# RMSNorm scale applied after the first products of a three-term float32 matmul kernel, and a wider transpose of its gated output

## The chip, the cores and the metric

The kernel runs on one core of one Trainium2 chip. The metric is the device time of one execution in microseconds (us). TensorE (PE) multiplies, VectorE (DVE) and ScalarE (ACT) work on tiles, GpSimd (POOL) and SyncE (SP) mostly issue DMAs here.

## The reference

One gMLP layer and a final RMSNorm on x of 1024 tokens x 2048 channels, all float32 (E = 4096):

```
h = rmsnorm(x, a_norm)
z = h @ w_in                       # 2048 x 12288 -> u | v | gate
u = gelu(u);  v = rmsnorm(gelu(v), v_gain)
sv = w_s mixes the 128 tokens of each chunk, 8 channel groups of 512, + b_s
x = x + (u * sv * silu(gate)) @ w_out      # 4096 x 2048
out = rmsnorm(x, final_norm)
```

## The kernel before

Both big products are Strassen products of 2x2 blocks: seven products p, each with a left factor from `A_OF` and a right one from `B_OF` (a block, or a sum or difference of two). Block 21 is half 1 of the tokens, column half 1, and so on. A float32 factor is split (L85) into hi (ACT rounds it to fp32r) and lo (DVE, the rest), and a product is three matmuls (L91: hi*hi, hi*lo, lo*hi).

The output columns of w_in come in 12 strips of two 512-column blocks: four for v, then eight with u and gate of one group. A strip has seven chains (one per p) of four steps; a step is 24 matmuls of 128x512 (two 128-rows of the inner dimension, four 128-token tiles, three terms), so a strip has 672. Then w_out: seven chains for each of two column pairs, eight steps each. The list `steps` sets this order on PE. At step i the program issues the loads of step i+3 and the sums and splits of step i+2 (`advance`, L367), so DVE and ACT run up to two steps ahead. Whatever a finished chain still needs goes into the lists `soon` and `later` and is popped a few at each step (`work`, L219). A scheduler then settles each engine's order; engines run their queues in order. Tiles come from pools of fixed size (`SLOTS`): a DMA or an instruction that writes a slot waits until its last reader is done.

The first strip makes the left factors for all strips from x and stores hi and lo to DRAM (`a_dram`); later strips load them. Before its first product, `load_x(0)` loads half of x (eight tiles of 512 KB), ACT squares it, DVE adds, a matmul with ones sums over channels, and `scale_x` makes 1/rms, a diagonal matrix of it, and by one more matmul the row `r_b`, by which (and by `g_in`) DVE multiplies each x tile in `h_block` (L171). The same for the other half follows after the first steps. Two chains accumulate into one set of PSUM banks (2 and then 4 and 7; 5 and then 3 and 6), of two sets; `end_of` (L414) takes a chain's banks over.

In a u-and-gate strip `apply_spatial` (L318) mixes the tokens, and `finish_y` (L346) transposes the gated result in 32x32 blocks, four 32-partition transposes for each 32 tokens of a chunk (L354), and stores y as [128, 4, tokens] per group and half. w_out's first column pair loads y, sums and splits it.

Of the kernel before, what the change touches and what calls it, by code (L numbers as in the profile page):

```python
# [10 lines left out]
ALU = mybir.AluOpType  # L11
# [12 lines left out]
FIRST_ORDER = (5, 3, 1, 2, 4, 6, 7)  # L24
# [8 lines left out]
def gmlp_kernel(ctx, tc, x, xT, g_in, w_in, gain, wsT, bsT, w_out, fnorm, out):  # L33
# [11 lines left out]
    NV = G // 2  # L45
    AHEAD, LOADS = 2, 3
# [30 lines left out]
    rx = const([P, NCH], "rx")  # L77
# [37 lines left out]
    y_dram = [[dram.tile([P, CB, HT], F32, tag=f"y{g}_{h}", name=f"y{g}_{h}") for h in range(2)] for g in range(G)]  # L115
# [45 lines left out]
    normal = set()  # L161

    def h_block(step, block, us=(0, 1)):

        key = ((block % 10 - 1) * JI + step[3], block // 10 - 1)
        t = hx[key]
        for u in us:
            if key + (u,) not in normal:
                normal.add(key + (u,))
                k = key[0] * 2 + u  # L170
                nc.vector.scalar_tensor_tensor(  # L171
                    out=t[:, u], in0=t[:, u], scalar=g_sb[:, k:k + 1], in1=r_b[:, key[1]],
                    op0=ALU.mult, op1=ALU.mult)
        return t

    def feed_first():

        step = steps[0]
        (a1, _, a2), (b1,) = A_OF[step[2]], B_OF[step[2]]
        aparts[0] = [slot("ax", f"a_{l}", F32R) for l in ("hi", "lo")]  # L180
        wparts[0] = [slot("hl", f"w_{l}", F32R) for l in ("hi", "lo")]
        split(load_w(step, b1), *wparts[0])
        hs = slot("sum", "a_sum")
        for u in range(2):
            t1, t2 = h_block(step, a1, (u,)), h_block(step, a2, (u,))
            nc.vector.tensor_tensor(out=hs[:, u], in0=t1[:, u], in1=t2[:, u], op=ALU.add)
            split(hs[:, u], *[t[:, u] for t in aparts[0]])
        for t, d in zip(aparts[0], a_dram[step[2], 0]):
            nc.gpsimd.dma_start(out=d, in_=t.bitcast(F32))

    def feed(i):
# [4 lines left out]
        first = kind == "in" and s == 0  # L196
        if first or (kind == "out" and s == 0):
            load = h_block if first else load_y
            raw = combine(A_OF[p], lambda b: load(step, b), "sum", "a_sum")


            out_j = j if kind == "out" else -1
            tag = "big" if (p == OUT_ORDER[0] and out_j >= JO - 4) or (p == OUT_ORDER[-1] and out_j == JO - 1) else "ax"
# [11 lines left out]

# [12 lines left out]

    ones = slot("ax", "ones")
# [4 lines left out]
    ss_x, r_ps = bank_set(1, "ss_x")  # L234
    r_b = slot("sum", "r_b")
    d_x = slot("ax", "d_x")
    dv = d_x.rearrange("p a (b c) -> p a b c", c=P)
    eyes = eye.rearrange("p (a c) -> p a c", a=1).broadcast_to([P, HCH, P])
    order_x = [jj for j in range(JI) for jj in (j, JI + j)]

    def load_x(h):

        for n, jj in enumerate(order_x):
            t = hx[jj, h] = slot("big", "x_t")
            nc.sync.dma_start(
                out=t, in_=xT[jj * 2 * P:(jj + 1) * 2 * P, h * HT:(h + 1) * HT].rearrange("(u p) c -> p u c", p=P))
            sq = slot("ax", "sq_x")
            nc.scalar.activation(out=sq, in_=t, func=AF.Square)
            nc.vector.tensor_tensor(out=sq[:, 0], in0=sq[:, 0], in1=sq[:, 1], op=ALU.add)
            nc.tensor.matmul(out=ss_x[:, h], lhsT=ones[:, 0, :P], rhs=sq[:, 0], start=n == 0, stop=n == len(order_x) - 1)  # L250

    def scale_x(h):

        cs = slice(h * HCH, (h + 1) * HCH)

        nc.vector.tensor_tensor(
            out=dv[:, h], in0=ss_x[:, h].rearrange("p (b c) -> p b c", c=P), in1=eyes, op=ALU.mult)
        nc.vector.tensor_reduce(out=ss_t[:, cs], in_=dv[:, h], axis=mybir.AxisListType.X, op=ALU.add)
# [3 lines left out]
        for n in range(HCH):
            nc.vector.tensor_scalar(
                out=dv[:, h, n], in0=eye, scalar1=rx[:, h * HCH + n:h * HCH + n + 1], scalar2=None, op0=ALU.mult)
        nc.tensor.matmul(out=r_ps[:, h], lhsT=ones[:, 0, :P], rhs=d_x[:, h], start=True, stop=True)
        nc.scalar.activation(out=r_b[:, h], in_=r_ps[:, h], func=AF.Copy)

    load_x(0)
    for i in range(LOADS):
        prefetch(i)  # L270
    scale_x(0)
# [18 lines left out]
    Q = 32  # L290
# [25 lines left out]
    def apply_spatial(g, half, n_set, prod):  # L316
# [29 lines left out]
    def finish_y(g, half, m, i, y):  # L346

        t, c = divmod(m, 2)
        if c == 0 and i == 0:
            yts[0] = slot("ax", "y_t").rearrange("p a (b c) -> p (a b) c", c=2 * P)  # L350
        yt = yts[0]
        yv = y[:, c].rearrange("t (b q c) -> t b q c", b=CB, q=P // Q)
# [4 lines left out]
        if c == 1 and i == P // Q - 1:  # L357
            nc.gpsimd.dma_start(out=y_dram[g][half][:, :, 2 * t * P:2 * (t + 1) * P], in_=yt)  # L358
            pairs_of_y[0] += 1

    pairs_of_y = [0]


    def products(i, banks, fresh, ms=range(4)):
# [263 lines left out]
```

## Time and profile before

| | us |
|---|---|
| median of 3 runs (2563.18 to 2563.37) | 2563.28 |
| profiled execution | 2561.8 |
| its span, first to last instruction | 2560.0 |
| PE busy / DVE / ACT / POOL in the span | 2514.0 / 1797.8 / 856.3 / 167.3 |

The profile counts an overlapping, pipelined PE as busy from the first matmul to the last of a run, so 98% hides slow stretches; the distance between the starts of matmuls shows those. The mean granted clock of TensorE was 0.995.

### The profile page before, as it was taken

The page shows a single profiled execution, that of the slowest core. Times are in us where ns is not written, and L with a number is a line of the kernel's source. Part 1 is how long each engine was busy: PE and PEld are TensorE (multiplying, and loading weights), DVE is VectorE, ACT ScalarE, POOL GpSimd, SP SyncE. Part 2 cuts the span into 40 slices and gives each one's busy share as a digit, 9 for nine tenths or more (in the row PEclk, how much of TensorE's full clock was granted, in tenths as well). Part 3 has the DMA queues.
Part 4 walks back from the last instruction along what each step waited for, and adds up shares of the span by engine and source line. Part 5 has one row for each costly group of instructions (what it writes and reads, how often), then busy time and mean ns, then how long its engine had stood idle before and what let it go on. Part 6 is the DMA issues. An engine that isn't in the chain of part 4 may idle for free.

```text
span 2560.0 us, 29690 instructions
## 1 busy us (share of the span) xinstructions
PE 2514.0 (98%) x10980; PEld 2062.0 (81%) x10980; DVE 1797.8 (70%) x2469; ACT 856.3 (33%) x1008; POOL 167.3 (7%) x290
## 2 busy tenths in 40 slices
PE   7999999999999999999999999999999999999998
PEld 4878888888888888888888888888888788888886
DVE  7974544545448869588595886958769855576795
ACT  4542332323324242232423324233243232232342
POOL 1210000000000000000000000000010110010010
PEclk8999999999999999999999999999999999999999
DMA  8897785958767685766858668586696875678885
GB/s 316 315 411 286 274 313 201 381 204 329 281 254 272 230 336 200 288 260 241 328 203 294 253 242 336 194 307 248 223 362 209 298 257 173 223 263 284 298 294 189
DMA packets 246784, 695.62 MB, mean 272 GB/s; under 512 B 21472, under 2 KB 21488, under 8 KB 246640
## 3 DMA queue, kind: packets, MB, share of 16 engines
q1 hardware_dynamic: 207552, 551.62, 59.7%
q0 software_dynamic: 39088, 142.11, 15.0%
q8 instruction: 87, 1.43, 0.2%
q14 instruction: 57, 0.47, 0.1%
HBM read 622.34 MB, written 71.30 MB: 271 GB/s over the span
## 4 chain that ended last, share of the span: by engine, by line
PE 76%; DVE 16%; issue 5%; DMA 2%; ACT 1%; POOL 0%; SPq 0%; POOLq 0%; ACTq 0%; DVEq 0%
PE m L94 19%; PE m L93 18%; PE m L95 18%; DVE y_t L354 8%; PE o L94 7%; PE o L93 7%; PE o L95 7%; DVE w_lo L89 3%; DVE w_sum L103 1%; DMA w_raw<-in_w_in 1%; DVE c L325 1%; DMA y_raw<-y 1%; DVE u L431 0%; DVE c L411 0%; ACT w_hi L88 0%
## 5 line engine op out<-in xcount | busy, mean ns | idle before, releaser
L93 PE MATMUL m<-w_hi,a_hi 128*128 128x512 f32 x2688 | 1048.5, 390 | 9.4 <-DVE u L431 4.8
L94 PE MATMUL m<-w_lo,a_hi 128*128 128x512 f32 x2688 | 1049.4, 390 | 4.5 <-DVE w_lo L89 4.5
L95 PE MATMUL m<-w_hi,a_lo 128*128 128x512 f32 x2688 | 1047.9, 390 | 0.2 <-DVE a_lo L89 0.2
L89 DVE TENSOR_TENSOR w_lo<-w_sum,w_hi 128x1024 fp32r<-128x1024 f32 x320 | 391.1, 1222 | 402.9 <-ACT w_hi L88 402.0
L88 ACT ACTIVATE w_hi<-w_sum 128x1024 fp32r<-128x1024 f32 x320 | 339.0, 1060 | 954.2 <-PE m L94 668.9
L93 PEld LDWEIGHTS m<-w_hi,a_hi 128*128 128x128 f32 x2688 | 505.8, 188 | 117.8 <-issue 6.6
L94 PEld LDWEIGHTS m<-w_lo,a_hi 128*128 128x128 f32 x2688 | 505.8, 188 | 114.8 <-DVE w_lo L89 9.8
L95 PEld LDWEIGHTS m<-w_hi,a_lo 128*128 128x128 f32 x2688 | 505.6, 188 | 105.8 <-DVE a_lo L89 0.9
L103 DVE TENSOR_TENSOR w_sum<-w_raw 128x1024 f32<-128x1024 f32 x320 | 389.7, 1222 | 100.5 <-DMA w_raw<-in_w_in 88.3
L94 PE MATMUL o<-w_lo,a_hi 128*128 128x512 f32 x896 | 349.6, 390 | 6.0 <-DVE w_lo L89 6.0
L93 PE MATMUL o<-w_hi,a_hi 128*128 128x512 f32 x896 | 348.7, 389 | 0.8 <-DVE o L575 0.8
L95 PE MATMUL o<-w_hi,a_lo 128*128 128x512 f32 x896 | 348.7, 389 | 0.0
L354 DVE STREAM_TRANSPOSE y_t<-c 32x128 f32<-32x128 f32 x1024 | 309.9, 303 | 15.1
L88 ACT ACTIVATE w_hi<-w_raw 128x1024 fp32r<-128x1024 f32 x128 | 135.9, 1061 | 451.2 <-PE m L94 348.7
L89 DVE TENSOR_TENSOR w_lo<-w_raw,w_hi 128x1024 fp32r<-128x1024 f32 x128 | 155.6, 1216 | 132.8 <-ACT w_hi L88 131.9
L94 PEld LDWEIGHTS o<-w_lo,a_hi 128*128 128x128 f32 x896 | 168.2, 188 | 44.0 <-DVE w_lo L89 9.3
L93 PEld LDWEIGHTS o<-w_hi,a_hi 128*128 128x128 f32 x896 | 168.2, 188 | 36.4 <-DVE o L575 1.5
L95 PEld LDWEIGHTS o<-w_hi,a_lo 128*128 128x128 f32 x896 | 168.2, 188 | 34.7
L88 ACT ACTIVATE a_hi<-a_sum 128x1024 fp32r<-128x1024 f32 (+1 forms) x61 | 63.7, 1044 | 146.4 <-DVE a_sum L103 137.0
L143 POOL DMA_DIRECT2D y_raw<-y x96 | 50.9, 531 | 467.0 <-DVE w_sum L103 245.6
L89 DVE TENSOR_TENSOR a_lo<-a_sum,a_hi 128x1024 fp32r<-128x1024 f32 (+1 forms) x61 | 73.3, 1202 | 10.1 <-ACT a_hi L88 10.1
L358 POOL DMA_DIRECT2D y<-y_t x32 | 23.1, 721 | 727.5 <-DVE y_t L354 727.5
(91 smaller groups left out, 1108.2 us busy)
## 6 DMA issues: line engine op xcount, KB each, us to landing
w_raw<-in_w_in SPq DMA_DIRECT2D x212, 512.0 KB, 6.7
w_raw<-in_w_out SPq DMA_DIRECT2D x192, 512.0 KB, 6.4
y_raw<-y POOLq DMA_DIRECT2D x96, 512.0 KB, 6.3
a_hi<-a_0h SPq DMA_DIRECT2D x77, 512.0 KB, 4.9
a_lo<-a_0l SPq DMA_DIRECT2D x77, 512.0 KB, 5.5
a_hi<-a_1h SPq DMA_DIRECT2D x77, 512.0 KB, 6.4
a_lo<-a_1l SPq DMA_DIRECT2D x77, 512.0 KB, 5.1
a_hi<-a_2h SPq DMA_DIRECT2D x77, 512.0 KB, 6.0
```

The source lines that it names most:

```text
L88: nc.scalar.activation(out=hi, in_=raw, func=AF.Copy)
L89: nc.vector.tensor_tensor(out=lo, in0=raw, in1=hi.bitcast(F32), op=ALU.subtract)
L93: nc.tensor.matmul(out=acc, lhsT=ah, rhs=bh, start=start, stop=False, skip_group_check=on)
L94: nc.tensor.matmul(out=acc, lhsT=ah, rhs=bl, start=False, stop=False, skip_group_check=on)
L95: nc.tensor.matmul(out=acc, lhsT=al, rhs=bh, start=False, stop=stop, skip_group_check=on)
L103: nc.vector.tensor_tensor(out=s, in0=a, in1=b, op=ALU.add if of[1] > 0 else ALU.subtract)
L143: nc.gpsimd.dma_start(out=yraw[key], in_=y_dram[g][block // 10 - 1][:, b:b + 2, :])
L325: nc.vector.scalar_tensor_tensor(out=y, in0=sv, scalar=bs_sb[:, g:g + 1], in1=y, op0=ALU.add, op1=ALU.mult)
L354: nc.vector.transpose(out=yt[q * Q:(q + 1) * Q, :, c * P + i * Q:c * P + (i + 1) * Q], in_=yv[i * Q:(i + 1) * Q, :, q, :])
L358: nc.gpsimd.dma_start(out=y_dram[g][half][:, :, 2 * t * P:2 * (t + 1) * P], in_=yt)
```

## The change

1. First strip: x is no longer multiplied by 1/rms. The left factors carry only `g_in` (ACT with a scale per partition, DVE scalar_tensor_tensor). 1/rms of a token (`rx`, one value per partition of a finished block) is the scale of the activation in `act`, which becomes two calls of 128x512 instead of one of 128x1024, in every strip. The squares are summed on DVE over 128x1024 and one matmul per half sums over partitions; the second half of x is loaded and squared during steps 2 to 13 (`first_step`).
2. The first strip runs the chains of one PSUM set in a row (5, 3, 6, then 1, 2, 4, 7), and blocks 11 and 21 of w are kept for several chains: 24 loads instead of 36.
3. `finish_y` transposes 128 partitions x 256 columns at once, two for each chunk; y lands in DRAM by channel, in eight DMAs of 128 KB per group and half (512-byte runs) instead of two of 512 KB. Tokens come out in another order; `split_y` puts them right while splitting, in runs of 32.

```diff
-FIRST_ORDER = (5, 3, 1, 2, 4, 6, 7)
+FIRST_ORDER = (5, 3, 6, 1, 2, 4, 7)
...
+    def split_y(raw, hi, lo):
+        rv_, hv = [t.rearrange("p u (q m t) -> p (u q) m t", m=HCH, t=Q) if t is raw else
+                   t.rearrange("p a b -> p (a b)").rearrange("p (m n t) -> p n m t", m=HCH, t=Q) for t in (raw, hi)]
+        nc.scalar.activation(out=hv, in_=rv_, func=AF.Copy)
...
+        nc.vector.tensor_tensor(out=lm, in0=rm, in1=hm.bitcast(F32), op=ALU.subtract)
...
-        cached = kind == "in" and (s > 0 or block == 22)
+        cached = kind == "in" and (s > 0 or block in (21, 22) or (block == 11 and p in (1, 2, 4)))
...
+    def feed_x(i):
+        step = steps[i]
...
+        if len(of) > 1 and of[0] % 10 != of[2] % 10:
+            raw2, hs = hx[key(of[2])], slot("sum", "a_sum")
+            for u in range(2):
+                nc.scalar.activation(out=hs[:, u], in_=raw2[:, u], func=AF.Copy, scale=g_of(of[2], u))
                 nc.vector.scalar_tensor_tensor(
+                    out=hs[:, u], in0=raw[:, u], scalar=g_of(of[0], u), in1=hs[:, u], op0=ALU.mult, op1=ALU.add)
...
+            for u in range(2):
+                nc.scalar.activation(out=hi[:, u], in_=raw[:, u], func=AF.Copy, scale=g_of(of[0], u))
+                nc.vector.scalar_tensor_tensor(
+                    out=lo[:, u], in0=raw[:, u], scalar=g_of(of[0], u), in1=hi[:, u].bitcast(F32),
+                    op0=ALU.mult, op1=ALU.subtract)
...
+    def square_x(jj, h):
+        sq = slot("ax", "sq_x")
+        nc.scalar.activation(out=sq, in_=hx[jj, h], func=AF.Square)
+        if h in sums:
+            nc.vector.tensor_tensor(out=sums[h], in0=sums[h], in1=sq, op=ALU.add)
...
+    def first_step(i):
+        if 2 <= i < 10:
+            load_x((i - 2), 1)
+        for h, at in enumerate((0, 8)):
+            n = i - at
+            for k in ((n,) if 0 <= n < 4 else (2 * n - 4, 2 * n - 3) if 4 <= n < 6 else ()):
+                square_x(order_x[k] if h == 0 else k, h)
+            if n == 6:
+                scale_x(h, h)
+    for j in range(JI):
+        load_x(j, 0)
+        load_x(JI + j, 0)
+        if j < LOADS:
+            prefetch(j)
...
-    def finish_y(g, half, m, i, y):
...
-        for q in range(P // Q):
-            nc.vector.transpose(
-                out=yt[q * Q:(q + 1) * Q, :, c * P + i * Q:c * P + (i + 1) * Q],
-                in_=yv[i * Q:(i + 1) * Q, :, q, :])
+    def finish_y(g, half, m, y):
...
+        for n in range(2):
+            nc.vector.transpose(out=yts[0][n][:, :, m * Q:(m + 1) * Q], in_=yv[:, n])
+        if m == HCH - 1:
+            yd = y_dram[g][half].rearrange("(n b c) t -> n c b t", n=2, c=Q)
+            for n in range(2):
+                for q in range(P // Q):
+                    nc.gpsimd.dma_start(out=yd[n, :, :, q * P:(q + 1) * P], in_=yts[0][n][q * Q:(q + 1) * Q])
...
-            nc.scalar.activation(out=d, in_=src, func=AF.Gelu_apprx_tanh if is_v or n == 0 else AF.Silu)
+            for c in range(2):
+                at = 2 * t + c
+                nc.scalar.activation(
+                    out=d[:, c], in_=src[:, c], func=AF.Gelu_apprx_tanh if is_v or n == 0 else AF.Silu,
+                    scale=rx[half][:, at:at + 1])
...
-                work()
+                if s == 0:
+                    first_step(i)
+                work(2.3 if s else 1.4)
```

The order on SP's DMA queue at the program's start, before (x_t are tiles of x, w_raw blocks of w_in, a_hi and a_lo the stored left factors; xN is N in a row):

```order
1 L245 DMA x_t<-in_xT 128x2x512 x8
2 L131 DMA w_raw<-in_w_in 128x2x512 x3
3 L245 DMA x_t<-in_xT 128x2x512 x8
4 L131 DMA w_raw<-in_w_in 128x2x512 x35
5 L155 DMA a_hi<-a_0h 128x1024
```

and now:

```order
1 L251 DMA x_t<-in_xT 128x2x512 x2
2 L144 DMA w_raw<-in_w_in 128x2x512
3 L251 DMA x_t<-in_xT 128x2x512 x2
4 L144 DMA w_raw<-in_w_in 128x2x512
5 L251 DMA x_t<-in_xT 128x2x512 x2
6 L144 DMA w_raw<-in_w_in 128x2x512
7 L251 DMA x_t<-in_xT 128x2x512 x2
8 L144 DMA w_raw<-in_w_in 128x2x512 x3
9 L251 DMA x_t<-in_xT 128x2x512
10 L144 DMA w_raw<-in_w_in 128x2x512
```

The loads of the first product's factors are now the first three, and half 1 of x comes between the loads of later steps.

DVE in the middle of the first strip, where it adds the squares of half 1 (sq_x, L259), folds the sum's halves (L266) for the one matmul that sums over channels, and prepares steps 15 to 17 (w_lo, a_lo; u is the take-over of chain 1), now:

```order
83 L259 TENSOR_TENSOR sq_x<-sq_x 128x1024
84 L186 SCALAR_TENSOR_TENSOR a_sum<-x_t,g_sb,a_sum 128x512
85 L259 TENSOR_TENSOR sq_x<-sq_x 128x1024
86 L90 TENSOR_TENSOR w_lo<-w_raw,w_hi 128x1024
87 L90 TENSOR_TENSOR a_lo<-a_sum,a_hi 128x1024
88 L266 TENSOR_TENSOR sq_x<-sq_x 128x512
89 L186 SCALAR_TENSOR_TENSOR a_sum<-x_t,g_sb,a_sum 128x512 x2
90 L271 TENSOR_TENSOR sq_x<-ss_x_0_953,ones 128x512
```

and PE at the matmul that waits for row 88 (ss_x), now:

```order
367 L105 MATMUL m_0_815<-w_hi,a_lo 128x512
368 L103 MATMUL m_1_816<-w_hi,a_hi 128x512
369 L104 MATMUL m_1_816<-w_lo,a_hi 128x512
370 L105 MATMUL m_1_816<-w_hi,a_lo 128x512
371 L268 MATMUL ss_x_0_953<-sq_x,ones 128x512
372 L103 MATMUL m_1_816<-w_hi,a_hi 128x512
```

Before, the sums of squares of half 1 stood much earlier on PE, within the first steps (step 1 of 28):

```order
36 L95 MATMUL m_1_332<-w_hi,a_lo 128x512
37 L250 MATMUL ss_x_168<-sq_x,ones 128x512
38 L94 MATMUL m_1_332<-w_lo,a_hi 128x512
39 L95 MATMUL m_1_332<-w_hi,a_lo 128x512
40 L93 MATMUL m_1_332<-w_hi,a_hi 128x512
41 L94 MATMUL m_1_332<-w_lo,a_hi 128x512
42 L250 MATMUL ss_x_168<-sq_x,ones 128x512 x7
```

So 369 of the first strip's 672 products now stand ahead of the second sum, and one matmul makes it.

DVE in the first u-and-gate strip, where the transposes begin (c is the gated product, sv the mixed tokens), before:

```order
387 L89 TENSOR_TENSOR w_lo<-w_sum,w_hi 128x1024
388 L325 SCALAR_TENSOR_TENSOR c_0_5561<-sv_0_0_5668,bs_sb,c_0_5561 128x512 x2
389 L325 SCALAR_TENSOR_TENSOR c_1_5562<-sv_0_1_5669,bs_sb,c_1_5562 128x512 x2
390 L354 STREAM_TRANSPOSE y_t<-c_0_5561 32x4x32 x16
391 L89 TENSOR_TENSOR v_lo<-v_raw,v_hi 128x1024
392 L89 TENSOR_TENSOR w_lo<-w_sum,w_hi 128x1024
393 L103 TENSOR_TENSOR w_sum<-w_raw 128x1024
394 L354 STREAM_TRANSPOSE y_t<-c_0_5561 32x4x32 x5
```

and now (the last rows of eight transposes in a row, 383 to 390):

```order
389 L376 STREAM_TRANSPOSE y_t_5736<-c_1_5586 128x8x32
390 L376 STREAM_TRANSPOSE y_t_5737<-c_1_5586 128x8x32
391 L90 TENSOR_TENSOR v_lo<-v_raw,v_hi 128x1024
392 L113 TENSOR_TENSOR w_sum<-w_raw 128x1024
393 L90 TENSOR_TENSOR w_lo<-w_sum,w_hi 128x1024
394 L483 TENSOR_TENSOR u_4853<-u_4853,m_0_4992 128x1024
```

The 64 transposes of half a group, which stood in runs between the other work, are eight in one run.

## Rows read from the trace of the kernel before

**Rows 1.** Stretches: us; busy PE, PEld, DVE, ACT, POOL; granted clock; DMA share; GB/s.
```profile
0.00:31.00 31.00, 12.92 (x18) 3.67 (x18) 15.38 (x25) 14.09 (x14) 3.73 (x10) 0.84 0.97 355
31.00:203.30 172.30, 166.01 (x690) 132.08 (x691) 154.00 (x163) 80.75 (x99) 36.05 (x65) 0.97 0.93 350
...
800.00:1900.00 1100.00, 1095.54 (x4819) 903.10 (x4818) 842.10 (x1445) 349.83 (x368) 37.32 (x60) 1.00 0.72 263
1900.00:2060.00 160.00, 153.95 (x671) 124.85 (x670) 143.55 (x226) 54.04 (x55) 23.71 (x39) 1.00 0.78 273
```
**Rows 2.** PE in order of time: start, us, line, tiles, [idle before <- what ended it].
```profile
31.10 0.79 PE L93 MATMUL m<-w_hi,a_hi 128*128 128x512 f32 x1 [4.06 <-ACT a_hi L88]
32.12 0.63 PE L93 MATMUL m<-w_hi,a_hi 128*128 128x512 f32 x1
32.54 0.63 PE L95 MATMUL m<-w_hi,a_lo 128*128 128x512 f32 x1
...
203.31 0.39 PE L93 MATMUL m<-w_hi,a_hi 128*128 128x512 f32 x1
...
355.63 0.39 PE L93 MATMUL m<-w_hi,a_hi 128*128 128x512 f32 x1
...
872.70 0.39 PE L93 MATMUL m<-w_hi,a_hi 128*128 128x512 f32 x1
873.70 0.50 PE L94 MATMUL m<-w_lo,a_hi 128*128 128x512 f32 x1 [0.62 <-DVE w_lo L89]
```
**Rows 3.** What PE waited for: us in total, times, longest us.
```profile
PE ss_x L250 <- DVE sq_x L249: 7.7, 6, 6.3
PE ss_x L265 <- DVE d_x L263: 7.1, 2, 6.4
PE o L94 <- DVE w_lo L89: 6.0, 6, 2.0
PE m L94 <- DVE w_lo L89: 4.5, 7, 0.7
```
**Rows 4.** ACT at the start, each waiting for the next 512 KB tile to land.
```profile
6.09 1.06 ACT L248 ACTIVATE sq_x<-x_t 128x1024 f32<-128x1024 f32 x1 [0.59 <-DMA x_t<-in_xT]
7.58 1.06 ACT L248 ACTIVATE sq_x<-x_t 128x1024 f32<-128x1024 f32 x1 [0.44 <-DMA x_t<-in_xT]
...
18.30 1.06 ACT L88 ACTIVATE w_hi<-w_raw 128x1024 fp32r<-128x1024 f32 x1 [0.30 <-DMA w_raw<-in_w_in]
19.65 1.06 ACT L88 ACTIVATE w_hi<-w_raw 128x1024 fp32r<-128x1024 f32 x1 [0.30 <-DMA w_raw<-in_w_in]
```
**Rows 5.** Granted clock (the number after POOL) around a stall, by stretch.
```profile
31.00:34.60 3.60, 3.50 (x8) 2.66 (x9) 3.60 (x7) 0.67 (x2) 0.64 (x1) 0.50 1.05 386
35.00:38.00 3.00, 3.00 (x14) 2.43 (x14) 3.00 (x5) 0.67 (x1) 0.54 (x1) 1.00 1.06 392
```
**Rows 6.** DVE in order of time: back-to-back instructions in the first strip.
```profile
69.92 1.41 DVE L171 SCALAR_TENSOR_TENSOR x_t<-x_t,g_sb,r_b 128x512 f32<-128x512 f32 x2
...
90.75 2.49 DVE L279 TENSOR_TENSOR c<-c,gain_b 128x512 f32<-128x512 f32 x4
...
118.83 2.35 DVE L89 TENSOR_TENSOR a_lo<-x_t,a_hi 128x1024 fp32r<-128x1024 f32 x2
```
**Rows 7.** Groups of instructions: tiles, count | busy us, mean ns of one | idle before.
```profile
L354 DVE STREAM_TRANSPOSE y_t<-c 32x128 f32<-32x128 f32 x1024 | 309.9, 303 | 15.1
L404 ACT ACTIVATE c<-m 128x1024 f32<-128x1024 f32 x48 | 48.9, 1019 | 56.2 <-PE m L95 56.2
L250 PE MATMUL ss_x<-sq_x,ones 128*128 128x512 f32 x32 | 18.1, 695 | 7.7 <-DVE sq_x L249 7.7
L358 POOL DMA_DIRECT2D y<-y_t x32 | 23.1, 721 | 727.5 <-DVE y_t L354 727.5
L531 ACT ACTIVATE o<-o,ro 128x512 f32<-128x512 f32 x16 | 10.7, 715 | 7.5 <-POOL ro L84 7.5
```
**Rows 8.** DVE at the start of w_out, waiting for y.
```profile
2014.69 1.23 DVE L103 TENSOR_TENSOR a_sum<-y_raw 128x1024 f32<-128x1024 f32 x1 [4.40 <-DMA y_raw<-y]
```

More of the change, by code (lines that the diff above doesn't have):

```diff
@@ L76, in gmlp_kernel @@
     ss_t = const([P, NCH], "ss_t")
-    rx = const([P, NCH], "rx")
+    rx = [const([P, HCH], f"rx{h}") for h in range(2)]
     m_all = const([P, NCH], "m_all")
@@ L114, in gmlp_kernel @@
     v_dram = [[dram.tile([P, HCH, C], F32, tag=f"v{g}_{h}", name=f"v{g}_{h}") for h in range(2)] for g in range(G)]
[L115 removed]
+    y_dram = [[dram.tile([C, HT], F32, tag=f"y{g}_{h}", name=f"y{g}_{h}") for h in range(2)] for g in range(G)]
     a_dram = {(p, j): [dram.tile([P, 2, HT], F32, tag=f"a{p}_{j}{l}", name=f"a{p}_{j}{l}") for l in "hl"]
@@ L195, in feed @@
         kind, s, p, j = step = steps[i]
[L196 to L203, printed above, removed]
+        if kind == "in" and s == 0:
+            feed_x(i)
+        elif kind == "out" and s == 0:
+            raw = combine(A_OF[p], lambda b: load_y(step, b), "sum", "a_sum")
+            tag = "big" if (p == OUT_ORDER[0] and j >= JO - 4) or (p == OUT_ORDER[-1] and j == JO - 1) else "ax"
             parts = [slot(tag, f"a_{l}", F32R) for l in ("hi", "lo")]
-            split(raw, *parts)
+            split_y(raw, *parts)
             aparts[i] = parts
-            if first:
-                for t, d in zip(parts, a_dram[p, j]):
-                    nc.gpsimd.dma_start(out=d, in_=t.bitcast(F32))
         elif kind == "out":
@@ L252, in scale_x, with load_x @@
-    def scale_x(h):
+    order_x = [jj for j in range(JI) for jj in (j, JI + j)]
+    sums = {}
+    def load_x(jj, h):
+        t = hx[jj, h] = slot("big", "x_t")
+        nc.sync.dma_start(
+            out=t, in_=xT[jj * 2 * P:(jj + 1) * 2 * P, h * HT:(h + 1) * HT].rearrange("(u p) c -> p u c", p=P))
+    def square_x(jj, h):
[3 more added lines that the diff above has]
+            nc.vector.tensor_tensor(out=sums[h], in0=sums[h], in1=sq, op=ALU.add)
+        else:
+            sums[h] = sq
@@ new lines, in scale_x @@
+    def scale_x(h, n_set):
+        sq = sums[h]
+        nc.vector.tensor_tensor(out=sq[:, 0], in0=sq[:, 0], in1=sq[:, 1], op=ALU.add)
+        ss_x = bank_set(n_set, f"ss_x{h}")[0]
+        nc.tensor.matmul(out=ss_x[:, 0], lhsT=ones[:, 0, :P], rhs=sq[:, 0], start=True, stop=True)
+        dv = sq[:, 1].rearrange("p (b c) -> p b c", c=P)
+        nc.vector.tensor_tensor(
+            out=dv, in0=ss_x[:, 0].rearrange("p (b c) -> p b c", c=P),
+            in1=eye.rearrange("p (a c) -> p a c", a=1).broadcast_to([P, HCH, P]), op=ALU.mult)
@@ L262, in scale_x @@
[L262 to L271, printed above, removed]
+        nc.gpsimd.tensor_tensor(out=rx[h], in0=m_all[:, cs], in1=mhalf[:, cs], op=ALU.pow)
@@ L327, in apply_spatial @@
         for m in range(HCH):
-            for part in range(P // Q):
-                later.append((1.2, lambda m=m, part=part: finish_y(g, half, m, part, prod[m // 2])))
+            later.append((0.8, lambda m=m: finish_y(g, half, m, prod[m // 2][:, m % 2])))
     def spatial_step(k, g, cs, n_set):
@@ L376, in advance @@
         feed(i + AHEAD)
-    feed_first()
-    for i in range(1, AHEAD):
+    for i in range(AHEAD):
         feed(i)
-    load_x(1)
-    scale_x(1)
     i = 0
@@ L432, in end_of, with last @@
                         out=cs["u"][t], in0=cs["u"][t], in1=banks[t], op=ALU.subtract)))
+                    if s == 0:
+                        def last(t=t):
+                            nc.vector.tensor_tensor(out=cs[22][t], in0=cs[22][t], in1=cs["u"][t], op=ALU.add)
+                            act(22, t, cs[22][t])
+                        soon.append((1.2, last))
+                elif s == 0 and p == 6:
+                    if t == 0:
+                        cs[22] = [slot("ax", f"c22_{t}") for t in range(2)]
+                    soon.append((0, lambda t=t: nc.scalar.activation(out=cs[22][t], in_=banks[t], func=AF.Copy)))
                 elif p in (4, 3):
```

105 lines of the change are left out of this document (40 added, 65 removed).

## The prediction

> **What bounds the kernel now.** I read the busy table by stretch first, then PE in order of time, then PE's waits, then ACT and DVE at the start.
>
> The busy table [rows 1] shows PE nearly full after 203.3 us: idle 1100.00 - 1095.54 = 4.5 us over most of the u-and-gate strips and 160.00 - 153.95 = 6.1 where w_out begins. DVE and ACT are far from full, so on PE nothing but the start and a few late tiles is to be had. PE in order of time [rows 2] gives the scale: strip 1 runs from 203.31 to 355.63, 152.3 us for 672 products, 0.2267 each, 5.44 a step. The first product starts at 31.10 and strip 1 only at 203.31, so the first strip takes 172.2 instead of 152.3. Up to there 203.3 - 152.3 = 51.0 us are lost; that is the big store. PE's waits [rows 3] name the small one: 4.5 us in 7 waits in the strips and 6.0 in 6 waits at w_out, all for a w_lo that DVE made late.
>
> **The start.** The factors of the first product are now the first three loads; three tiles of 512 KB have landed at 7.58, and from there they come 1.35 apart (18.30 to 19.65 [rows 4]). ACT then makes w_hi (1.06, as in rows 4) and half of a_hi (about 0.6, half of it and a little more): first product at about 9.5. The wait for sums, scale and row falls away. [...]
>
> **The first strip, by three sums.**
> PE alone: 9.5 + 1.9 + 152.3, and two sums of squares at 18.1 / 16 = 1.1 each [rows 7] (sixteen now): 165.9.
>
> DVE: PE can't pass the second sum of squares before DVE's row 88 in the order, the last of 55 operations of 128x1024, 34 of scalar_tensor_tensor, nine of 128x512 and two small ones. Back to back they come 1.13, 0.67 and 0.62 apart (from runs of two, two and four [rows 6]); the two small ones I put at 0.7 together: 62.2 + 22.8 + 5.6 + 0.7 = 91.3. DVE can begin when x's second tile is there (6.09 [rows 4]) and ACT has scaled half of it (0.715 [rows 7]), at 6.8, and reaches row 88 at 98.1 plus whatever it idles, I. Behind that matmul stand 303 of 672 products, 68.7 us, and its own 1.1: the strip ends at 167.9 + I. PE would be there at 9.5 + 1.9 + 369 x 0.2267 + 1.1 = 96.1, so it waits there for 2 + I, with everything after it queued behind.
>
> DMA gives I. By the order the loads up to step 11's pair are 30 tiles, and by then about 20 tiles of left factors are stored: 50 tiles, of which 11 have landed at 19.65; 39 x 1.35 = 52.7, so the pair lands at 72.3. Sum, hi and lo (1.13 + 1.06 + 1.13) make its w_lo 75.6. Without idling DVE would have been through that row at 6.8 + 59.1 = 65.9. So I is up to 9.7 if all these stores go first, and 0 if they lag behind the loads. ACT's extra work (two scaled copies of at most 0.715 a step) may add some, since it hands tiles back and forth with DVE; I allow 13. I take 8, nearer to the DMA sum, because the DMA share was already 0.97 in both early stretches [rows 1]. The strip ends at 175.9 instead of 203.3: 27.4 us less. After step 12 loads fall to one or none a step (the kept blocks), so the DMA can't hold the rest.
>
> The chains now follow each other on one bank set at 5-3, 3-6, 2-4 and 4-7. ACT or DVE reads the first banks while PE still writes the last ones, so I count nothing; at most the reading of one bank pair, 1.0 each [rows 7], if ACT is late. That belongs to I.
>
> **The activations in halves.** 96 calls of 1.02 (48 stand in rows 7) become 192 of at most 0.715, the price of half a tile with a scale per partition [rows 7]: up to 96 x 0.41 = 39 us on ACT, busy a third of the span. A chain's banks are needed again only a chain later (four steps, 21.8 us) outside the first strip, so it costs nothing there; with that cover gone it would be 0.4 us a call.
>
> **The transposes.** 1024 of 0.303 us [rows 7], 310 us, become 128. The trace has none of 128 x 256. From below it can't cost less than 0.30, the same instruction with half the columns; from above, eight times as many 32x32 blocks at the same price each make 2.42. I take twice 0.303, since each partition has twice the columns: 0.61, 78 us in all, 232 off DVE. Only the late w_lo tiles turn that into time. Each such wait costs a little more than it shows: 872.70 to 873.70 is 1.00, 0.77 over the pace, for a wait of 0.62 [rows 2]. So 4.5 + 6.0 + 13 x 0.15 = 12.5 us are at stake. The longest (2.0) comes after DVE waited 4.40 for y from DRAM [rows 8], and may stay: 10.5. The eight transposes in one run take 4.9 us before the next w_lo; with two steps of lead, 10.9, PE doesn't see them.
>
> **Stores and splits of y.** POOL issues 128 DMAs instead of 32, at most 0.72 each [rows 7]: 69 us more, on an engine busy 61 us in these stretches [rows 1]. If the 512-byte runs take the DMA twice as long, 16.8 MB at 263 GB/s [rows 1] become 64 us more over 1250, on a share of 0.72. No PE work waits for either, since y is read strips later, except at the end of the last group; I count 0, and 3 us there at worst. The 56 splits that reorder tokens cost 1.13 each if runs of 32 are as good as one run; a bound above is 2.37 ns per column, the transposes' price, 2.42. Then DVE would need 1.3 more in each of 56 steps, which are 5.44 long and hold five operations; some 10 us would come out at PE. I take 0, as all of DVE's rows on plain elementwise work lie at one price per column. [...]
>
> **The sum.** 2560.0 - 27.4 - 10.5 = 2522.1 for the span; the execution lies 1.8 above its span, and the median of the runs 1.5 above the profiled one: about 2525.
>
> **Rivals.**
> *The first strip stays short of tiles.* For it: DMA share 0.97 there, and five tiles a step in steps 8 to 11. With I = 25 it ends at 193, 10 us earlier; with 10.5 from the transposes, 2543. Against it: 12 loads fewer in the strip, and after step 12 one a step or none.
> *The w_lo waits stay or come back elsewhere.* Runs of eight could be late where sixteen short ones were not: only the start's 27.4 remains, 2536. Against it: at w_out, where the longer waits are, DVE is busy 143.6 of 160 us [rows 1], and the transposes are what goes from it.
> *The transposes cost by the block.* At 2.42 the DVE total stays 310 us, but in runs of eight: 19.4, with the four gating operations ahead and the next sum and split behind some 25.5 us without a w_lo, where PE has the step it is in and two more, 16.3. It would stall about 9 us for each of sixteen halves, 147, and end near 2563 - 27 + 147 = 2683: slower. It decides from 8t + 6.1 > 16.3, t = 1.3 us. All transposes in the trace have 32 partitions, so no row excludes it; but DVE's other operations take 128 partitions at 1.1 to 1.2 ns a column [rows 6], under the 2.4 of a transpose of 32, so partitions cost it nothing elsewhere: 0.04. [...]
>
> **How the numbers follow.** Forecast 0.71, with its own range 2515 (I = 0 and all 12.5 back) to 2534 (I = 13, 7 back); strip short of tiles 0.13; waits stay 0.12; by the block 0.04. The range goes down to 2512 (PE's own sum, 165.9, with all 12.5 back and part of the 1.9 for the clock) and up to 2543, the first rival's time, half of which lies beyond; it leaves out about 0.15. A median within 0.2% (5 us) of 2563 counts as no change: only a strip that gains nothing and waits that stay would give that, 0.01. Faster 0.95, slower 0.04.
>
> **What would show it.** First product at 9 to 11 us; strip 1's first product at 168 to 181; a PE wait for the sum of squares (L266) near 96 to 106 us; DVE idle before w tiles between 20 and 75; transposes at about 0.6; no PE wait for w_lo after 800 us but one at w_out. I am wrong if strip 1 starts after 190, if a transpose takes over 1.3 us, or if PE waits anew in the u-and-gate strips.

## The result, and the profile after

| | before | after |
|---|---|---|
| median, us | 2563.32 (2563.18 to 2564.04) | 2527.68 (2527.18 to 2528.85) |
| span of the profiled execution, us | 2560.0 | 2525.5 |
| first product of the program, us | 31.10 | 10.49 |
| first product of strip 1, us | 203.31 | 184.25 |
| from there to the last product, us | 2345.9 | 2329.3 |
| from the last product to the end, us | 10.7 | 11.9 |

The ratio is 0.9861, 95% interval 0.9844 to 0.9878: faster by 35.6 us, where 2525 was forecast and 2527.7 lies within the range. The two terms behind it did not come out as written. The first strip gave 19.1 us and not 27.4, the later strips and w_out 16.6 and not 10.5; the tail took 1.2 back. 19.1 + 16.6 - 1.2 = 34.5 is the difference of the spans. The 19.1 is all start: the first product comes 20.6 us earlier, and from it to strip 1 it takes 173.8 us where it took 172.2. The forecast had the strip itself at 166.4.

The busy table of the kernel after answers [rows 1]; its columns are the same, the granted clock stands behind POOL.

```profile
10.50:16.90 6.40, 6.40 (x14) 4.75 (x15) 5.66 (x7) 4.19 (x6) 1.67 (x3) 1.00 1.04 383
...
34.00:37.30 3.30, 3.30 (x9) 2.55 (x8) 3.30 (x5) 2.51 (x5) 1.90 (x4) 0.50 1.05 395
65.00:71.70 6.70, 0.08 (x1) 0.00 (x0) 5.71 (x5) 3.62 (x5) 5.21 (x2) 0.73 1.04 408
71.70:74.90 3.20, 3.16 (x8) 2.48 (x9) 1.42 (x2) 3.20 (x6) 0.54 (x1) 0.50 1.05 390
...
800.00:1900.00 1100.00, 1100.00 (x4855) 911.14 (x4854) 624.63 (x671) 370.38 (x435) 80.48 (x142) 1.00 0.74 266
1900.00:2060.00 160.00, 160.00 (x708) 132.53 (x707) 108.02 (x101) 52.80 (x58) 33.29 (x58) 1.00 0.81 279
```

Below, PE is full: 1100.00 of 1100 and 160.00 of 160, where it lacked 4.5 and 6.1. DVE fell from 842 to 625 us in the long stretch. Above, PE stands still from 65.0 to 71.7, and the granted clock is 0.50 (half clock below), as in [rows 5], from 34.0 to 37.3 and behind the standstill. In the first row products start 0.43 us apart, as they do from 34.3 to 36.9 at 0.50, though the granted clock of the first row is 1.00.

PE in order of time, and then what it waited for, answer [rows 2, 3].

```profile
10.49 0.80 PE L103 MATMUL m<-w_hi,a_hi 128*128 128x512 f32 x1 [10.49 <-ACT a_hi L89]
...
32.15 0.49 PE L103 MATMUL m<-w_hi,a_hi 128*128 128x512 f32 x1 [1.88 <-ACT a_hi L89]
...
40.33 0.46 PE L103 MATMUL m<-w_hi,a_hi 128*128 128x512 f32 x1
...
43.93 0.50 PE L103 MATMUL m<-w_hi,a_hi 128*128 128x512 f32 x1 [1.52 <-ACT u L447]
...
71.74 0.79 PE L103 MATMUL m<-w_hi,a_hi 128*128 128x512 f32 x1 [6.66 <-ACT c L428]
...
184.25 0.39 PE L103 MATMUL m<-w_hi,a_hi 128*128 128x512 f32 x1
```
```profile
PE m L103 <- ACT a_hi L89: 12.4, 2, 10.5
PE m L103 <- ACT c L428: 6.7, 1, 6.7
PE m L103 <- ACT u L447: 1.5, 1, 1.5
PE o L103 <- DVE o L611: 0.8, 1, 0.8
PE m L105 <- DVE a_lo L90: 0.6, 1, 0.6
PE m L103 <- DVE u L457: 0.2, 1, 0.2
```

Both lines on w_lo are gone, and both on the sums of squares. Chain 3 takes over chain 5's first banks at 40.33 and the others at 43.93. The largest wait behind the start is new: at 71.74 chain 6 wants the bank set of chain 3, which ACT still reads. The next rows are of three engines around that wait, POOL, then DVE, then ACT.

```profile
65.71 4.68 POOL L278 TENSOR_TENSOR rx<-m_all,mhalf 128x4 f32<-128x4 f32 x1
...
119.21 1.05 POOL L278 TENSOR_TENSOR rx<-m_all,mhalf 128x4 f32<-128x4 f32 x1
```
```profile
64.78 0.16 DVE L276 TENSOR_SCALAR m_all<-ss_t 128x4 f32<-128x4 f32 x1
64.86 1.22 DVE L113 TENSOR_TENSOR w_sum<-w_raw 128x1024 f32<-128x1024 f32 x1
65.99 1.22 DVE L195 TENSOR_TENSOR a_sum<-x_t 128x1024 f32<-128x1024 f32 x1
67.13 1.22 DVE L113 TENSOR_TENSOR w_sum<-w_raw 128x1024 f32<-128x1024 f32 x1
68.26 1.22 DVE L90 TENSOR_TENSOR w_lo<-w_sum,w_hi 128x1024 fp32r<-128x1024 f32 x1
69.51 1.23 DVE L195 TENSOR_TENSOR a_sum<-x_t 128x1024 f32<-128x1024 f32 x1
```
```profile
67.24 1.28 ACT L428 ACT_TABLE_LOAD   x1
70.42 2.42 ACT L428 ACTIVATE c<-m,rx 128x512 f32<-128x512 f32 x4 [1.90 <-POOL rx L278]
```

Read them upwards: PE waits for the activation of block 12, that for 1/rms of half 0, and that is POOL's power of 4 numbers a partition. The same instruction took 1.05 us for half 1, beside an operation of DVE that reads one operand from PSUM (u, from 118.36). Here DVE ran operations with two operands from SBUF, back to back, beside it.

Of the groups in [rows 7], the transposes and their stores now read:

```profile
L376 DVE STREAM_TRANSPOSE y_t<-c 128x256 f32<-128x256 f32 x128 | 43.6, 406 | 0.0
L381 POOL DMA_DIRECT2D y<-y_t x128 | 74.0, 586 | 409.1 <-DVE y_t L376 405.4 <-issue 1.9 <-DVE w_lo L90 1.8
```

310 us of transposes became 44.

### The profile page after: what moved, and what is told of

It reads as the page before. It is cut to its first block, busy times and chain, and to the rows that moved or that the text cites. A ratio compares the mean times of both kernels' runs of the same rounds, so it can differ in the third digit from the quotient of the medians.

```text
span 2525.5 us, 28995 instructions
## 1 busy us (share of the span) xinstructions
PE 2491.7 (99%) x10948; PEld 2058.9 (82%) x10948; DVE 1526.9 (60%) x1560; ACT 896.0 (35%) x1144; POOL 221.1 (9%) x386
## 3 DMA queue, kind: packets, MB, share of 16 engines
q0 software_dynamic: 40624, 142.12, 15.2%
## 4 chain that ended last, share of the span: by engine, by line
PE 96%; issue 2%; POOL 1%; DVE 0%; DMA 0%; ACT 0%; SPq 0%; POOLq 0%; ACTq 0%
PE m L103 24%; PE m L104 23%; PE m L105 23%; PE o L103 8%; PE o L105 8%; PE o L104 8%; PE sv L104 1%; PE sv L105 1%; PE sv L103 1%; DMA x_t<-in_xT 0%; POOL rx L278 0%; DVE w_sum L113 0%; DVE w_lo L90 0%; ACT w_hi L89 0%; ACT sq_o L536 0%
## 5 line engine op out<-in xcount | busy, mean ns | idle before, releaser
L381 POOL DMA_DIRECT2D y<-y_t x128 | 74.0, 586 | 409.1 <-DVE y_t L376 405.4
L428 ACT ACTIVATE c<-m,rx 128x512 f32<-128x512 f32 x96 | 60.4, 683 | 55.9 <-PE m L105 54.0
L96 ACT ACTIVATE a_hi<-a_sum 128x1024 fp32r<-128x1024 f32 x40 | 42.3, 1058 | 100.0 <-DVE a_sum L113 100.0
L319 POOL DMA_DIRECT2D v_raw<-v x32 | 17.4, 544 | 661.3 <-DVE ws_hl L334 646.0
```

The source lines that it names most:

```text
L96: nc.scalar.activation(out=hv, in_=rv_, func=AF.Copy)
L319: nc.gpsimd.dma_start(out=spatial["v", c], in_=v_dram[g][h][:, 2 * t:2 * t + 2])
L381: nc.gpsimd.dma_start(out=yd[n, :, :, q * P:(q + 1) * P], in_=yts[0][n][q * Q:(q + 1) * Q])
L428: nc.scalar.activation(out=d[:, c], in_=src[:, c], func=AF.Gelu_apprx_tanh if is_v or n == 0 else AF.Silu, scale=rx[half][:, at:at + 1])
```

## Experiments

All medians stand against 2527.7 for the kernel after; the kernel before, run beside them each time, gave 2561.7 to 2562.7. No edited kernel's times lay more than 2.5 us apart. The kernel after itself was timed beside a 2563.3 of the kernel before, so differences of about 1 us are not read.

**The layout of y undone (e1_old_y).** The hunks of `finish_y`, `split_y`, `products` and the loads of y and w_out are those of the kernel before; all else is after.
```diff
-            split_y(raw, *parts)
+            split(raw, *parts)
-                later.append((0.8, lambda m=m: finish_y(g, half, m, prod[m // 2][:, m % 2])))
+                for part in range(P // Q):
+                    later.append((1.2, lambda m=m, part=part: finish_y(g, half, m, part, prod[m // 2])))
```


> The kernel after with only the layout of y undone: the transposes into 32 partitions, the old stores and loads of y and the old split are back; the scale on finished blocks and the chain order of the first strip stay. Theory: between the first product of strip 1 and the last product the trace gained 16.6 us, all of it from the vector engine's load, so this kernel should lose just that: about 2527.7 + 16.6 = 2544 us, with its first strip ending near 184 as after the change, and the waits for w_lo back. Rival: those waits went because the scale moved off the vector engine (fewer operations in the first strip, other slots free), not because of y: then this kernel stays below 2532.

2546.0 us (2545.1 to 2546.6), 18.3 more. Strip 1 starts at 185.12, and the w_lo lines of [rows 3] are back, in total almost to the digit:
```profile
PE o L104 <- DVE w_lo L90: 6.0, 4, 3.4
PE m L104 <- DVE w_lo L90: 4.4, 7, 0.6
```
The rival (the waits went with the scale) is out. From strip 1 to the last product it takes 2348.8 us, 19.5 more than the kernel after and 2.9 more than the kernel before: the longest wait is now 3.4 and not 2.0, and behind it, at 2002.50, the granted clock is 0.50 and 13 products start 0.43 apart.

**The layout of y alone (e2_only_y).** The same hunks, put into the kernel before.


> The kernel before with the new layout of y alone. Theory: the two gains add up, so this one gains the 16.6 us alone: about 2563.3 - 16.6 = 2546.7 us, with the first strip ending near 203 as before. Rival: the parts need each other: above 2555 if the transposes alone do not take the waits away, below 2540 if the new layout helps the first strip as well.

2547.6 us (2545.9 to 2548.2), 14.7 less than the 2562.3 of before. From strip 1 to the last product it takes 2329.33 us, as the kernel after to the hundredth; but the first strip ends at 205.18, 1.9 later than before, and the tail is as long as in the kernel after (11.8). So the part works alone. The two parts add to within 4 us: singly they give 14.7 and, by e1, 16.3, which is 31.0 of the 34.7 that they give together. In the profiles 5.6 lacks (15.2 and 13.7 of 34.5), and the 1.9 here and the 2.9 of e1 are most of it; why the first strip ends later here is not shown.

**The transposes twice (e12_twice).**
```diff
-            nc.vector.transpose(out=yts[0][n][:, :, m * Q:(m + 1) * Q], in_=yv[:, n])
+            for _ in range(2):
+                nc.vector.transpose(out=yts[0][n][:, :, m * Q:(m + 1) * Q], in_=yv[:, n])
```


> The kernel after with each of the 128 transposes of y done twice (0.41 us each, 52 us more on VectorE, into the same tile). Theory: after the change VectorE is busy for 625 of 1100 us and no w_lo wait is left, so what the transposes cost now is hidden whole: within 1 us of 2527.7; the price of a transpose no longer enters. Rival: VectorE still ends last at the steps that hold the transposes: each strip of the 8 with y gains back part of the old 0.6 us waits and w_out its own, 3 to 10 us more.

2528.9 us (2528.3 to 2529.5), 1.2 more, a little over the bound. The profile puts 0.8 of it into the first strip (strip 1 at 185.07), where there are no transposes, and 0.3 behind it; there PE has no new wait, with DVE 36 us busier in the first of two stretches:
```profile
800.00:1900.00 1100.00, 1100.00 (x4854) 910.85 (x4853) 660.40 (x777) 371.22 (x436) 80.08 (x141) 1.00 0.75 267
1900.00:2060.00 160.00, 159.97 (x706) 132.16 (x705) 112.08 (x115) 52.70 (x58) 34.40 (x59) 1.00 0.81 278
```
What is left of the transposes is hidden, but for the 0.3 at most.

**Nothing waits for 1/rms (e6_no_scale).**
```diff
-            for c in range(2):
-                at = 2 * t + c
-                nc.scalar.activation(
-                    out=d[:, c], in_=src[:, c], func=AF.Gelu_apprx_tanh if is_v or n == 0 else AF.Silu,
-                    scale=rx[half][:, at:at + 1])
+            nc.scalar.activation(out=d, in_=src, func=AF.Gelu_apprx_tanh if is_v or n == 0 else AF.Silu)
```


> The kernel after with the activations done without the scale of tokens, both chunks in one call (1/rms of x is left out of the computation; it is still worked out, but nothing waits for it). Theory: the wait at 71.74 is for 1/rms; it shrinks to about 1.5 us and the first strip's half clock behind it goes: about 2521 us, at most 1 us less by the fewer ScalarE calls. Rival: the wait comes from ScalarE's own work at that place (the table load of 1.28 us and the activations): then it stays above 4 us and the time at 2526 to 2528.

2520.5 us (2519.7 to 2521.6), 7.2 less. The line on c in PE's waits is gone altogether, though the table load stayed: the wait was for 1/rms. POOL's power still took 4.68 us, now with nobody behind it.

**The bank freed without the scale (e3_drain).**
```diff
-                    soon.append((0, lambda t=t, block=block: act(block, t, banks[t])))
+                    if s == 0 and p == 3:
+                        soon.append((0, lambda t=t: nc.scalar.activation(out=cs[12][t], in_=banks[t], func=AF.Copy)))
+                        later.append((0, lambda t=t: act(12, t, cs[12][t])))
+                    else:
+                        soon.append((0, lambda t=t, block=block: act(block, t, banks[t])))
```


> The kernel after, with block 12 of the first strip copied out of its banks unscaled by ScalarE at the end of chain 3, and the activation with the scale of tokens done from SBUF a step later. Theory: the 6.66 us wait at the turnover from chain 3 to chain 6 (and the half clock behind it) is the wait for 1/rms of half 0; without it the turnover costs about what that from chain 5 to 3 costs (1.5 us), so 5.1 us of wait and about 1.5 us of half clock go: about 2521 us. Rival: ScalarE, held in order by the same activation a step later, holds up the splits of the next tiles instead, and the wait only moves: 2526 to 2528.

2523.5 us (2523.3 to 2523.8), 4.2 less and not 6.6. The wait at 71.74 and the half clock behind it are gone, the ACT rival is out; but DVE, which was level with PE at the second sum of squares (PE's wait for it was 0.19), now ends last at new places:
```profile
PE m L104 <- DVE w_lo L90: 1.9, 2, 1.3
PE m L103 <- ACT u L447: 1.6, 1, 1.6
PE m L103 <- DVE u L457: 1.1, 1, 1.1
```

**Why the power takes 4.68 us (e13_gap).** Three copies from a bank are put on DVE behind the mean of each half; they feed nothing.
```diff
         nc.gpsimd.tensor_tensor(out=rx[h], in0=m_all[:, cs], in1=mhalf[:, cs], op=ALU.pow)
+        for _ in range(3):
+            nc.vector.tensor_copy(out=sq[:, 1], in_=ss_x[:, 0])
```


> The kernel after with three copies of the sum of squares from its bank (128x512, one operand, from PSUM) put on VectorE behind the mean, which feed nothing; they come to stand between the operations with two operands from SBUF that ran back to back beside GpSimd's power of half 0. What is read is that power's duration. Theory: GpSimd is held while VectorE runs operations with two operands from SBUF; beside a copy from PSUM it gets on, so its power of half 0 lasts 1 to 2.7 us and no longer 4.68, and the wait at the turnover from chain 3 to 6 falls to about 4 to 5 us; the time changes by less than 3 us either way, since the copies cost VectorE some 2 us. Rival: the 4.68 us have nothing to do with what VectorE runs beside: they stay at 4 us or more, and the wait at 6.5 or more.

2525.7 us (2525.4 to 2526.5), 2.0 less with 4 us more work for DVE (six copies of 0.68). POOL, then DVE, at the same place:
```profile
65.82 1.87 POOL L278 TENSOR_TENSOR rx<-m_all,mhalf 128x4 f32<-128x4 f32 x1
```
```profile
64.96 0.68 DVE L280 COPY sq_x<-ss_x 128x512 f32<-128x512 f32 x1
65.56 1.21 DVE L113 TENSOR_TENSOR w_sum<-w_raw 128x1024 f32<-128x1024 f32 x1
66.69 0.68 DVE L280 COPY sq_x<-ss_x 128x512 f32<-128x512 f32 x1
67.30 1.21 DVE L195 TENSOR_TENSOR a_sum<-x_t 128x1024 f32<-128x1024 f32 x1
```
The power lasts 1.87 and PE's wait fell to 4.79: both as the theory had it. The ends say more. The power ended at 67.69, 0.92 us behind the two-operand operation that the second copy follows (65.56 + 1.21). In the run e7 below, where DVE stood still from 64.07 for want of a tile, it lasted 3.02 and ended 0.91 behind that. In the kernel after it ended at 70.39, 0.91 behind the end of the w_lo of 68.26, the fourth operation of the run, and it lasted the same 4.68 in e3 and e6. So in these three traces it ended 0.91 to 0.92 behind the end of an operation of DVE: in e13 and e7 of the one behind which DVE didn't go on with two operands from SBUF, in the kernel after of one behind which it did (a_sum at 69.51). Why it missed three ends there and took the fourth is not shown.

**Probes on POOL (e9_probe).** One more power of a constant a step, 28 in all.
```diff
+        nc.gpsimd.tensor_tensor(out=probe, in0=pone, in1=mhalf[:, :HCH], op=ALU.pow)
```


> The kernel after with one more small power of a constant (128x4) on GpSimd at each of the 28 steps of the first strip, which feeds nothing. Theory: GpSimd's small operation lasts about 1.05 us by itself, and 2 to 5 us where VectorE runs operations back to back that read two operands from SBUF; the probes sort by what VectorE does beside them. Rival: the 4.68 us at 65.71 came of what stood on GpSimd just ahead of it (the issue of a transfer): then the probes behind an issue are long whatever VectorE does, and the others short.

2540.7 us, one run. That it costs 13 us was not foreseen: the probes wait for nothing, so POOL ran through 15 of them in a row (24.04 to 49.0) with the stores of the split tiles behind them; ACT waited 11.2 us at 52.97 for a store to land, and PE 6.4 for a w_hi. That is 7.1 of the 13, in the first strip; the rest lies behind it and is not explained. Four of them:
```profile
24.04 1.03 POOL L285 TENSOR_TENSOR probe<-pone,mhalf 128x4 f32<-128x4 f32 x1
...
34.85 5.13 POOL L285 TENSOR_TENSOR probe<-pone,mhalf 128x4 f32<-128x4 f32 x1
40.06 3.52 POOL L285 TENSOR_TENSOR probe<-pone,mhalf 128x4 f32<-128x4 f32 x1
43.66 1.01 POOL L285 TENSOR_TENSOR probe<-pone,mhalf 128x4 f32<-128x4 f32 x1
```
From 42.7 to 54.3 DVE stood still, and the probes then took 1.01 to 1.03; the longest lay beside six DVE operations back to back, behind another probe and no issue, and the four right behind an issue took 1.03 to 1.73: the rival is out. But the theory said too much: most probes beside a busy DVE took 1.0 to 1.4 as well (the median of all is 1.06). So beside two-operand operations in a row some probes lasted 1.0 to 1.4 and others up to 5.13; what decides it is not shown.

**1/rms without POOL (e10_sqrt).**
```diff
-        nc.gpsimd.tensor_tensor(out=rx[h], in0=m_all[:, cs], in1=mhalf[:, cs], op=ALU.pow)
+        nc.vector.reciprocal(out=m_all[:, cs], in_=m_all[:, cs])
+        nc.scalar.activation(out=rx[h], in_=m_all[:, cs], func=AF.Sqrt)
```


> The kernel after with 1/rms of x worked out without GpSimd: a reciprocal of 128x4 on VectorE and the square root of it on ScalarE (table loads of about 1.3 us come with it). Theory: of the 6.66 us wait at the turnover from chain 3 to 6, 4.68 us are GpSimd's power, held up by VectorE's operations beside it; in its place stand some 0.3 us on VectorE and ScalarE and one or two table loads, so the wait shrinks by about 2 to 3.5 us and the time to some 2524 to 2526 us. Rival: the wait is for the sum and its column order on VectorE, and GpSimd's time is only how the profile draws it: the wait stays within 1 us of 6.66 and the time at 2527 to 2529.

2528.0 us (2527.6 to 2528.6); the wait is 6.29. By its numbers the rival won, but the run doesn't tell the two apart: POOL's 4.68 are gone, and on ACT a w_hi and two table loads stand in their place, so that the activation starts at 70.40, where it started at 70.42.
```profile
66.51 1.06 ACT L89 ACTIVATE w_hi<-w_sum 128x1024 fp32r<-128x1024 f32 x1 [3.52 <-DVE m_all L278]
67.58 1.28 ACT L279 ACT_TABLE_LOAD   x1
68.88 0.21 ACT L279 ACTIVATE rx<-m_all 128x4 f32<-128x4 f32 x1
69.10 1.28 ACT L429 ACT_TABLE_LOAD   x1
70.40 2.42 ACT L429 ACTIVATE c<-m,rx 128x512 f32<-128x512 f32 x4
```

**The clock at the start (e5_warm).**
```diff
+    scratch = bank_set(1, "warm")[0]
+    for k in range(8):
+        nc.tensor.matmul(out=scratch[:, 0], lhsT=ones[:, 0, :P], rhs=ones[:, 0], start=True, stop=True)
```


> The kernel after with 8 matmuls of a tile of ones, which feed nothing, put on TensorE ahead of the first product (they fit in the wait for the first tiles). Theory: the products from 10.49 to 16.9 us ran at the lower granted clock because TensorE had been idle before; with work ahead of them they run at full speed from the start: some 2.8 us less, about 2525 us. Rival: those products wait for the pieces of the split or for tiles, not for the clock: less than 0.8 us gained, 2527 to 2528.

2527.9 us (2527.3 to 2528.9): nothing, as the rival had it, though for another reason. The products did start 0.23 apart (0.43 after the change), so work ahead of them did away with the slow pace, though the granted clock of the stretch is 1.00 in both traces. But the tiles of step 3 land when they land: PE came there sooner and waited longer, 3.64 and not 1.88.
```profile
12.00 0.39 PE L104 MATMUL m<-w_lo,a_hi 128*128 128x512 f32 x1
12.23 0.40 PE L105 MATMUL m<-w_hi,a_lo 128*128 128x512 f32 x1
...
32.39 0.80 PE L103 MATMUL m<-w_hi,a_hi 128*128 128x512 f32 x1 [3.64 <-ACT a_hi L89]
```

**Early loads put off (e7_defer).**
```diff
-    nc.gpsimd.dma_start(out=ws_sb, in_=wsT.rearrange("g q p -> q g p"))
...
                     first_step(i)
+                    if i == 7:
+                        load_gains()
+                        nc.gpsimd.dma_start(out=ws_sb, in_=wsT.rearrange("g q p -> q g p"))
```


> The kernel after with the loads of ws_sb and of the first gains (512 KB each, in flight among the first tiles) put off to step 7 of the first strip. Theory: the tiles of step 3 land late (26.3 and 30.1 us) because the transfers before them fill the DMA engines at some 385 GB/s; 1 MB less lets them land some 2.6 us earlier, so the stall at 32 us (2.5 us in all) and the half clock behind it (about 1.4 us) mostly go: about 2524 us. Rival: the stall is the order of the splits on ScalarE and VectorE, or the tiles come through another queue's order: within 0.8 us of 2527.7.

2522.8 us (2522.5 to 2523.7), 4.9 less; the profiled run, the slowest of the four, shows 3.7 of it. The trace shows that the edit put off one load and not two: the load of ws_sb still stands at 2.60, the program's start. So it is the load of the gains alone, 512 KB, that did this; it stood at 17.61 in the kernel after, where the gains are first read at 77 us. POOL in the kernel after, then here:
```profile
17.61 0.54 POOL L418 DMA_DIRECT2D gain_b<-in_gain  x1
```
```profile
2.60 0.91 POOL L507 DMA_DIRECT2D ws_sb<-in_wsT  x1
...
60.33 0.54 POOL L418 DMA_DIRECT2D gain_b<-in_gain  x1
```
What an early ws_sb costs is not tested. The stall at 32.15 and the half clock behind it are gone, and chain 3 has its first banks at 37.07 instead of 40.33 and the others at 40.80 instead of 43.93:
```profile
37.07 0.50 PE L102 MATMUL m<-w_hi,a_hi 128*128 128x512 f32 x1 [1.31 <-ACT u L449]
...
40.80 0.50 PE L102 MATMUL m<-w_hi,a_hi 128*128 128x512 f32 x1 [1.61 <-ACT u L449]
```

**All three, and two of them (e8_all, e11_two).** The edits of e3, e5 and e7 together; then those of e3 and e7. In both, too, ws_sb is loaded at 2.6 us and only the gains are put off.


> The three edits together on the kernel after: block 12 copied out unscaled, 8 matmuls ahead of the first product, the loads of ws_sb and of the first gains put off. Theory: they sit at three places of the first strip, so their gains add: 6.6 + 2.8 + 3.9 = 13.3 us, about 2514 us. Rival: an earlier start runs into the same late tiles (what the first edit gives back at the start is lost at the next step): 2519 to 2522.

> The kernel after with two edits: block 12 copied out unscaled, and the loads of ws_sb and of the first gains put off; without the matmuls ahead of the first product. Theory: those matmuls gave nothing (alone 2527.9, what they gave at the start went into a longer wait for the tiles of step 3), so this is as fast as the three together, 2519.6 within 1 us. Rival: with the tiles earlier the clock at the start counts as well: then this is 2521.5 or more.

2519.6 us (2519.6 to 2520.4) and 2520.3 (2519.8 to 2521.2). The sum of 13.3 was too much (8.1 came, within the rival's 2519 to 2522), since e5 gives nothing and e3 less than thought: 4.2 + 4.9 = 9.1 singly. Strip 1 starts at 176.84 with the work ahead of the first product and at 177.02 without: by that it is worth 0.2, and the difference of the medians, 0.7, is too small to read. The two edits beat the kernel after by 7.4 us and the kernel before by 41 (ratio 0.9837, 0.9823 to 0.9852).

## Why the prediction was right, and where not

**The start.** Predicted 9.5, measured 10.49. A table load of 1.28 us on ACT, which the prediction left out, now stands at 6.34, behind the wait for its first tile, where before it stood at 0.79, under that wait. No run shows the 1.9 us that the prediction's sums count for a slow pace at the start; the trace of the kernel after shows 14 products 0.43 apart, where 0.2267 is the pace of strip 1, some 2.8 us more.

**The first strip: the sum by DVE held, its idle time I did not.** Strip 1 was to start at 168 to 181 and started at 184.25. The step said that PE can't pass the second sum of squares before DVE, at 98.1 + I, and that the strip ends at 167.9 + I, with I = 8 and 13 allowed. That matmul ran at 113.68, which makes I 15.6, and 167.9 + 15.6 = 183.5 against 184.25. DVE's busy time from 6.8 to 113.5 was 92.1 for 91.3 predicted; the rest is idle time, 14.6. The rows of DVE give it: 1.6 because of the start, 1.1 in three short waits up to 17.3, 2.3 + 3.7 + 2.7 between 18 and 31 us waiting for ACT on late tiles of steps 2 and 3, and 2.75 ahead of 73.48. The 8.7 for tiles is about what I = 8 stood for. The DMA sum had up to 9.7 for all tiles up to step 11, but the shortage came at once, in the first 32 us, with loads in flight that no early step needs; without the gains (e7) DVE's three waits there are 2.3 + 2.8 + 0.6. The 2.75 is of the second missed kind: ACT, in order, stood in front of the next a_hi with an activation that wanted 1/rms.

So the wait forecast for 96 to 106 us, 2 + I long, was 0.19 when it came: PE had lost the time already, at 32 and at 65, and there the two engines were level. **The step that failed** is "ACT or DVE reads the first banks while PE still writes the last ones, so I count nothing; at most the reading of one bank pair, 1.0 each". At the turnover from chain 3 to 6 the wait and the half clock behind it took 8.4 us of PE. The step counted reading a bank, not what the reading needs: the change makes the drain of chain 3 wait for the chain of sum, matmul, reduction and power of half 0, and POOL's power, which the prediction gave no price, was 4.68 of the 6.66. e6 shows that the wait is for 1/rms (7.2 us), and e13 that the power is shorter with copies from PSUM between DVE's operations (1.87 for 4.68). Freeing the bank alone (e3) gave only 4.2, since DVE, level with PE, then ends last. One of the two-operand operations beside the power is 1.22 long, and the power stood through several of them; what holds it is not shown.

**The later strips.** 10.5 predicted, 16.6 measured; e1 and e2 put it on y's layout alone. 12.5 us were at stake by the sum of the shown waits; but a step that ends late costs beyond its own wait. Strips of 158.9 us became 157.8: a wait of 0.62 cost 1.1, with the short delays around it, where 0.77 was counted. And the wait of 2.0 that was to stay behind y's landing went too. The transpose of 128 x 256 took 0.406 us: nearer to the lower bound, 0.30, than to the 0.61 taken, so the rival by the block (2683) is out by a factor of six. At 0.61 the result would have been about the same: e12, at 0.81 for two, lost 0.3 there.

**Halves, stores, splits of y.** Counted at nothing, and nothing is to be seen: PE doesn't wait after 184.25 us but for 0.8 at the end, and e2, which has no halves, takes the same 2329.33 from strip 1 on. ACT's busy time rose from 856.3 to 896.0, about the 39 allowed. The reordering split took 1.22 on DVE and 1.06 on ACT, the price of a plain one.

**The two errors.** 8.3 us too much for the first strip and 6.1 too little behind it: that the total came within 2.7 is luck, since two errors of opposite sign met. The tail's 1.2 us more comes with y's layout (10.8 in e1, 11.8 in e2); by what is not shown.

## What to carry to other kernels

Where a scale is moved from the operands to the result, the drain of the first results inherits the wait for it (6.66 us here): follow that chain, engine by engine, to the bank that the next chain needs, or copy the bank out unscaled. Clock or waits won ahead of a late tile are given back at that tile (in e5 the wait there grew from 1.88 to 3.64); look first at what else is in flight. A forecast of when an engine is done needs its idle time as much as its work, and so the waits that the change itself adds.

## What was not expected of the hardware

- A power of 128x4 on POOL lasts 1.01 to 1.05 us with DVE at rest (e9, and the kernel before at 22.95), 1.05 beside an operation with one operand from PSUM, and 1.0 to 5.13 beside DVE operations with two SBUF operands back to back. Adding 4 us of copies from PSUM to DVE made the kernel 2.0 us faster.
- DVE's transpose costs 0.303 us for 32x128 and 0.406 for 128x256: eight times the blocks for a third more time.
- The granted clock fell to 0.50 at 34.0, behind waits of 1.88 and 0.64, and at 68 within the wait of 6.66; PE then ran some 3 us at it, which cost about 1.6 us beside each wait. It stayed at 1.00 behind the wait of 1.52 at 43.93, and over the stretch of 0.6 us waits in the kernel before [rows 1]. At the start products were as slow with a granted clock of 1.00 in the rows.
